# A gated DeltaNet scan whose small products go to all four quarters of TensorE's array, in two-bank PSUM tiles

## The chip, the cores and the metric

The kernel runs on one core of one Trainium2 chip. The metric is the device time of one execution in microseconds (us), as the median of the runs.

## What is computed

The reference is two layers of a mixer block with 1024 columns, over a context of 256 tokens and a latent stream of 1024. In each layer one normalised input goes through one input projection into four groups (a DeltaNet with short convolutions, a gated convolution, a Conformer convolution, a chunked spatial-gating MLP); their gated outputs are joined and go through one output projection with a gated residual. The change touches the DeltaNet: four heads of 64 columns, run forward and backward over chunks of 64 tokens (16 for the latent stream, 4 for the context). With the state S of a head and direction, a chunk does

```
x  = sg0 * (K S) + nk
v  = T x
o  = sg1 * (Q S) - A v
S  = sg2 * S + K' (sg3 * v)
```

K, Q and K' are the chunk's keys and queries, T the inverse of a triangular 64x64 matrix, A the causal weights of the chunk, sg0 to sg3 gates, nk the negated values. The context's last state starts the latent scan of its layer.

## The kernel before

The program is not written in the order in which it runs. Class `Program` records every operation, `estimate` (line 140) gives each a cost, and `schedule` (line 255) puts the operations of each engine into one fixed order: of those that are ready it takes the one with the smallest number of recording, less a boost (800 for the scan, `AHEAD_SCAN`; 600 for convolutions, 300 for the rest of the DeltaNet, 0 for the inversion). Since all operations are issued by one helper, every row of the profile shows line 214, and an operation is known by its tiles.

Most of TensorE's time goes to the dense projections (`mm3`, tiles `mm`): each is three products of 128x128 by 512 columns in a reduced fp32 format, on high and low parts (`hh`, `hl`). What the scan leaves of TensorE is filled with them.

The DeltaNet of a stream runs in stages, `gdn` (line 1310) first:

- `norms` (1417): sums of squares per token and head, by 64x1 products.
- `pair_matrices` (1444): for two chunks a call the products K K and Q K of both directions, masked. A call stores its `zd` (three matrices, one DMA each) and its `at` (two DMAs) to DRAM on SP's queue. There are 8 calls for a latent stream and 2 for a context, 20 in all.
- `invert` (1488): loads 32x32 blocks of `zd` (tile `u`), inverts them by a row loop on VectorE, and stores `zb`. It runs in two groups of chunks for the latent stream.
- `prep` in `scan` (1540): for four chunks, loads `zb`, `zd` and `at`, and makes the full 64x64 inverses T with 32x32 products (tile `ax<-b,b`).
- `scan` (1520): the loop over the chunks. The four scans of the program (context, latent; layer 0, layer 1) have 4, 16, 4 and 16 steps.
- `gdn_out` (1677), then the output projection (`out_item`), with weights from `load_w_out` (1717).

In the scan, the 128 partitions hold two heads' halves p, and an index hh picks the pair of heads; d is the direction. So each product of the formula is a group of eight 64x64 by 64 products, over d, hh and p. Half p of the rows writes half p of the PSUM partitions:

```
for d, hh, p in each:
    self.mm(A[half[p], 0, d, hh, :], st.qk[hh][half[p], 1, tok(d)], S[half[p], d, hh, :])
```

That is the two quarters on the diagonal of the array, in turn. A group in fp32 stands in the trace as 16 instructions, for each product is two passes. A step runs K S (`sc<-s,u`) into bank A; two VectorE operations make x; T x (`sc<-x,u`) goes into A too; a copy on ScalarE makes v1, VectorE makes v2; K' v2 (`sc<-v,u`) goes into its own bank, and VectorE adds it to gs into S. Beside that chain stand Q S and A v1 (into a bank Bk), VectorE's `at`, `ot` and `gs`, and the addition to the output. `psx` (517) hands out single PSUM banks to everything else: four banks of the scan and the bank `ax` in turn, or `ax` alone while a scan runs.

Of the kernel before, what the change touches and what calls it, by code (L numbers as in the profile page):

```python
# [16 lines left out]
P = 128  # L17
# [62 lines left out]
class Program:  # L80
# [13 lines left out]
    def __init__(self, nc):  # L94
        self.nc = nc
        self.ops, self.slots, self.hist, self.tileops, self.bufs = [], {}, {}, {}, {}
        self.masks, self.boost, self.joined = {}, 0, None
        self.tensor, self.vector = Engine(self, "PE", nc.tensor), Engine(self, "DVE", nc.vector)
        self.scalar, self.gpsimd = Engine(self, "ACT", nc.scalar), Engine(self, "POOL", nc.gpsimd)
        self.sync = Engine(self, "SP", nc.sync)  # L100
# [39 lines left out]
    def estimate(self, eng, method, out, ins, args, kw):  # L140
# [45 lines left out]
    def add(self, calls):  # L186
# [29 lines left out]
        for w, aps in ((False, ins), (True, outs)):  # L216
            for a in aps:
                name = a.name
                if "PSUM" in str(a.space):
                    reg, bank = (0, 128, 1), True  # L220
                elif name in self.slots or "DRAM" in str(a.space):
                    if name not in self.slots and not name.startswith(self.DRAM_OWN):
                        continue
                    reg, bank = self.region(a), False
                else:
                    continue
# [237 lines left out]
class Block:  # L464
    def __init__(self, es, tc, ins, out, dbg=None):
        self.tc, self.nc, self.i, self.out = tc, Program(tc.nc), ins, out
        pool = lambda name, bufs, **kw: es.enter_context(tc.tile_pool(name=name, bufs=bufs, **kw))
        self.cp = pool("cp", 1)
        self.sp = pool("sp", 2)
        self.hp = pool("hp", 1)  # L470
        self.pools = {k: pool(k + "p", n) for k, n in CAPS.items()}
        self.cnt = {k: 0 for k in CAPS}
        self.dp = pool("dp", 1, space=DRAM)
        self.mmp = pool("mm", 3, space=PSUM)
        self.ax = pool("ax", 1, space=PSUM)
        self.sc = pool("sc", 1, space=PSUM)
        self.n = self.xi = self.scanning = 0
        self.W = Weave()

# [44 lines left out]
    def scan_bank(self, k, shape):  # L524
        return self.nc.own(self.sc.tile(shape, F32, tag=f"sc{k}", name=self.nm("sc")), f"sc{k}", 1)

# [723 lines left out]
    def group_a_gates(self, st):  # L1250
# [3 lines left out]
        def ev(j):  # L1254
            def go(ps, b0, n):
# [4 lines left out]
                def put():  # L1260
                    for q in range(2):
                        r = q * P + j * HD
                        nc.sync.dma_start(st.gd[r:r + HD, b0:b0 + n], g[q * HD:(q + 1) * HD])
# [44 lines left out]


    def gdn(self, st, need_q, states):  # L1310
        nc, l, n = self.nc, st.l, st.n
# [30 lines left out]

        pe = self.psx([P, 6, m])
        for d in range(2):
            self.mm(pe[:, d], self.Rm[d], g[:, d])
            self.mm(pe[:, 2 + d], self.Lm[d], g[:, d])
# [19 lines left out]
        st.nk = V("nk", 1)[:, 0]  # L1366
        nc.vector.tensor_tensor(st.nk, nq[:, 1], rn[:, 1], ALU.mult)
        wd = S("wd", [P, 2, 32])[:, :, :m]
# [21 lines left out]
        for hh in range(2):  # L1390
            self.shuffle(st.nkv, st.pad, hh, n)
        if not st.ctx:
# [24 lines left out]
    def norms(self, st, kind, nq):  # L1417

        nc, n = self.nc, st.n
        pq = self.psx([P, 2 * n])  # L1420
        for b0, nb in st.blocks:
            for hh in range(2):
                yield self.room("b")
# [3 lines left out]
                for c in range(nb // TC):  # L1427
                    e = (b0 // TC + c) * 2 + hh
                    for p in range(2):
                        s = slice(p * TC, (p + 1) * TC)  # L1430
                        self.mm(pq[s, e:e + 1], sq[s, c * TC:(c + 1) * TC], self.ones[s])
                self.free("b")
        nc.vector.tensor_scalar(nq[:, kind], pq, EPS, None, ALU.add)

    def shuffle(self, dst, src, hh, n):

        for q in range(4):
            p, a = q // 2, q % 2
            v = src[q * CH:(q + 1) * CH, hh, 1:n * TC + 1].rearrange("p (c u j) -> p u c j", u=2, j=CH)
            for u in range(2):  # L1440
                r = p * TC + u * CH
# [78 lines left out]
    def scan(self, st, S, need_o):  # L1520
# [62 lines left out]

        pend = None

        def out(s, i, bank, v1, at):
            AT = ATs[s // G % 2]
            for d in range(2):
                for hh in range(2):
                    e = 2 * (G - 1 - i if d else i) + hh  # L1590
                    for p in range(2):
                        self.mm(bank[half[p], 1, d, hh, :], AT[half[p], d, e], v1[half[p], d, hh, :])

        def out_add(s, i, bank, v1, at):
            oc = st.o[:, two_of(s, n - 1 - s)].rearrange("p d (h e) -> p d h e", h=2)
# [6 lines left out]
            if not fresh:  # L1602
                self.two(oc, oc, ot, ALU.add)

        yield from prep(0)
        side = None
        for s in range(n):
# [4 lines left out]
            first, last = st.ctx and s == 0, s == n - 1 and not st.ctx  # L1612
            each = [(d, hh, p) for d in range(2) for hh in range(2) for p in range(2)]
            sg = lambda k: st.sg[:, s, k].unsqueeze(3).to_broadcast(sh)
            tok = lambda d: slice(cc[d] * TC, (cc[d] + 1) * TC)
            A = self.scan_bank(0, [P, 2, 2, 2, HD])
            nk = st.nkv[:, two_of(*cc)].rearrange("p d (h e) -> p d h e", h=2)
            if first:
                x = nk
            else:  # L1620
                for d, hh, p in each:
                    self.mm(A[half[p], 0, d, hh, :], st.qk[hh][half[p], 1, tok(d)], S[half[p], d, hh, :])
# [12 lines left out]
            nc.joined = None if first else ready  # L1635
            for d, hh, p in each:
                self.mm(A[half[p], 1, d, hh, :], Ts[j % 2][half[p], d, 2 * (G - 1 - i if d else i) + hh, :], x[half[p], d, hh, :])
            at = None
            if need_o:
                Bk = self.scan_bank(2, [P, 2, 2, 2, HD])  # L1640
                if not first:
                    for d, hh, p in each:
                        self.mm(Bk[half[p], 0, d, hh, :], st.qk[hh][half[p], 0, tok(d)], S[half[p], d, hh, :])
            if not last:
# [3 lines left out]
            if need_o:  # L1648
                v1 = self.small("v1", sh)
                nc.scalar.copy(v1, A[:, 1])  # L1650
                if not first:
                    at = self.small("at", sh)
                    nc.vector.tensor_tensor(at, Bk[:, 0], sg(1), ALU.mult)
                pend = (s, i, Bk, v1, at)
            yield STEP[1]
            if not last:
                nc.joined = ready
                Sp = self.scan_bank(1, sh)
                for d, hh, p in each:
                    self.mm(Sp[half[p], d, hh, :], st.kst[half[p], cc[d], hh * HD:(hh + 1) * HD], v2[half[p], d, hh, :])  # L1660
                if first:
                    nc.vector.tensor_copy(S, Sp)
                else:
                    nc.vector.tensor_tensor(S, gs, Sp, ALU.add)
            if side:
# [6 lines left out]
        if need_o:  # L1672
            out(*pend)
            out_add(*pend)
        self.scanning -= 1
# [41 lines left out]
    def load_w_out(self, l, after, keep):  # L1717
# [5 lines left out]
        for i, k in enumerate((4, 5, 6, 7, 2, 3, 0, 1)):  # L1723
            yield lambda: self.cnt["u"] + 1 + keep() <= CAPS["u"]
            r = raw[:, i % 2]
            if k < 2:
                for h in range(2):
                    r0 = (2 * h + k) * HD
                    nc.sync.dma_start(r[h * HD:(h + 1) * HD], self.i["w_out"][l, r0:r0 + HD, :])
# [403 lines left out]
```

## Time and profile before

| | |
|---|---|
| median of 3 runs | 1384.72 us (1384.66 to 1385.25) |
| the profiled execution | 1382.8 us, of which its span 1381.1 us |
| TensorE, weight loads, VectorE, ScalarE busy | 94%, 76%, 71%, 39% of the span |
| mean granted TensorE clock | 0.969 |

The profile is of one execution. Its span goes from the first instruction to the last. Matmuls overlap, and the busy time of one is its whole length, so that a TensorE shown busy can still have room. A latent scan of layer 0 stands at about 456 to 570 us and that of layer 1 at 1109 to 1206 us.

### The profile page before, as it was taken

The page shows a single profiled execution, that of the slowest core. Times are in us where ns is not written, and L with a number is a line of the kernel's source. Part 1 is how long each engine was busy: PE and PEld are TensorE (multiplying, and loading weights), DVE is VectorE, ACT ScalarE, POOL GpSimd, SP SyncE. Part 2 cuts the span into 40 slices and gives each one's busy share as a digit, 9 for nine tenths or more (in the row PEclk, how much of TensorE's full clock was granted, in tenths as well). Part 3 has the DMA queues.
Part 4 walks back from the last instruction along what each step waited for, and adds up shares of the span by engine and source line. Part 5 has one row for each costly group of instructions (what it writes and reads, how often), then busy time and mean ns, then how long its engine had stood idle before and what let it go on. Part 6 is the DMA issues. An engine that isn't in the chain of part 4 may idle for free.

```text
span 1381.1 us, 27009 instructions
## 1 busy us (share of the span) xinstructions
PE 1299.9 (94%) x10992; PEld 1047.1 (76%) x10992; DVE 986.2 (71%) x2102; ACT 539.9 (39%) x903; POOL 11.9 (1%) x76
## 2 busy tenths in 40 slices
PE   6887899999999999999999999998999888999997
PEld 4886778987778666678887788987777776788886
DVE  3888959999869755753466659899788866753554
ACT  4877433254644221321244355343475121231221
POOL 1000000000000000000000000000000000000000
PEclk9988899999999999999999999999899989999999
DMA  9748232322485566561333341523237533122831
GB/s 306 213 109 242 58 74 70 86 47 61 111 203 145 151 198 190 185 184 54 109 115 111 100 113 51 128 54 88 66 99 178 121 80 100 49 76 96 269 82 56
DMA packets 308465, 166.74 MB, mean 121 GB/s; under 512 B 148254, under 2 KB 292982, under 8 KB 308342
## 3 DMA queue, kind: packets, MB, share of 16 engines
q1 hardware_dynamic: 308342, 165.03, 43.3%
q8 instruction: 86, 1.41, 0.4%
q14 instruction: 37, 0.30, 0.1%
HBM read 124.32 MB, written 35.42 MB: 116 GB/s over the span
## 4 chain that ended last, share of the span: by engine, by line
PE 60%; DVE 15%; DMA 14%; ACT 3%; issue 3%; SPq 3%; ACTq 0%; DVEq 0%
PE mm L214 45%; PE sc L214 11%; DVE u L214 8%; DMA x<-u 6%; PE ax L214 5%; DVE b L214 3%; SPq L214 3%; DMA r<-in_w_in 3%; DVE w L214 2%; DMA u<-in_w_out 2%; ACT u L214 1%; DMA whh<-in_w_ada 1%; DMA whl<-in_w_ada 1%; DMA u<-in_x 1%; DMA b<-zb 1%
## 5 line engine op out<-in xcount | busy, mean ns | idle before, releaser
L214 PE MATMUL mm<-hh,w 128*128 128x512 f32 x1664 | 541.4, 401 | 1.7 <-ACT w L214 1.2
L214 PEld LDWEIGHTS mm<-hh,w 128*128 128x128 f32 x1664 | 311.8, 190 | 82.0 <-issue 16.5
L214 PE MATMUL mm<-hl,w 128*128 128x512 f32 x832 | 334.3, 402 | 0.0
L214 PE MATMUL mm<-u,w 128*128 128x512 f32 (+1 forms) x1320 | 261.5, 356 | 1.6 <-ACT g L214 1.1
L214 PEld LDWEIGHTS mm<-u,w 128*128 128x128 f32 x1320 | 220.0, 193 | 35.3 <-ACT g L214 1.7
L214 DVE SCALAR_TENSOR_TENSOR u<-u,pv,u 128x1024 f32<-128x1024 f32 (+1 forms) x172 | 201.9, 1182 | 1.0
L214 PEld LDWEIGHTS mm<-hl,w 128*128 128x128 f32 x832 | 157.9, 190 | 40.7 <-issue 9.3
L214 ACT CAST w<-r 128x1024 fp32r<-128x1024 f32 x88 | 92.5, 1051 | 214.4 <-PE mm L214 159.2
L214 ACT ACT_TABLE_LOAD x94 | 120.6, 1283 | 17.7 <-DMA zd<-b 5.9
L214 DVE TENSOR_TENSOR w<-r,w 128x1024 fp32r<-128x1024 f32 x88 | 107.2, 1218 | 27.3 <-ACT w L214 26.8
L214 DVE TENSOR_TENSOR u<-u,b 128x256 f32<-128x256 f32 (+25 forms) x246 | 89.3, 378 | 26.5 <-DMA u<-in_x 16.3
L214 PE MATMUL mm<-u,u 128*128 128x256 f32 (+1 forms) x384 | 56.5, 299 | 9.8 <-ACT u L214 4.2
L214 DVE TENSOR_TENSOR b<-u 128x108 f32<-128x108 f32 (+21 forms) x180 | 56.5, 323 | 7.0 <-DMA u<-zd 3.8
L214 PEld LDWEIGHTS mm<-u,u 128*128 128x128 f32 x384 | 51.2, 200 | 12.8 <-DVE u L214 5.0
L214 ACT ACTIVATE b<-u 128x512 f32<-128x512 f32 (+1 forms) x71 | 42.5, 609 | 40.4 <-DVE u L214 29.4
L214 PEld LDWEIGHTS sc<-v,u 64*64 64x64 f32 x1184 | 40.3, 138 | 16.0 <-DVE v L214 9.9
L214 PEld LDWEIGHTS sc<-s,u 64*64 64x64 f32 x1168 | 40.6, 141 | 15.1 <-DVE s L214 4.5
L214 PE MATMUL sc<-s,u 64*64 64x64 f32 x1168 | 47.3, 230 | 2.3 <-DVE u L214 1.7
L214 PE MATMUL sc<-v,u 64*64 64x64 f32 x1184 | 46.6, 226 | 2.5 <-DVE v L214 1.3
L214 PE MATMUL mm<-u,hh 128*128 128x272 f32 x256 | 48.5, 289 | 0.0
L214 ACT ACTIVATE b<-sc,mod,modG 128x128 f32<-128x128 f32 x76 | 30.9, 459 | 44.5 <-PE sc L214 26.9
L214 PE MATMUL sc<-dg,u 128*128 128x128 f32 x248 | 38.2, 311 | 8.7 <-issue 4.7
(271 smaller groups left out, 1451.8 us busy)
## 6 DMA issues: line engine op xcount, KB each, us to landing
r<-in_w_in SPq DMA_DIRECT2D x90, 512.0 KB
u<-in_w_ada SPq DMA_DIRECT2D x16, 1024.0 KB
u<-in_x SPq DMA_DIRECT2D x16, 512.0 KB
r<-ylat SPq DMA_DIRECT2D x16, 512.0 KB
zd<-b SPq DMA_DIRECT2D x60, 128.0 KB
ylat<-g SPq DMA_DIRECT2D x24, 256.0 KB
u<-in_w_out SPq DMA_DIRECT2D x12, 512.0 KB
at<-b SPq DMA_DIRECT2D x36, 128.0 KB
```

Of the source, the lines that this page charges most:

```text
L214: op.alts[e] = ((lambda fn=fn, ar=ar, k=k: fn(*ar, **k)), cost, table)
```

## The change

It does six things, all in the DeltaNet and the recording layer.

1. In the scan the heads with hh = 1 change sides: half p of the rows writes half 1 - p of the partitions for K S, Q S, T x and A v1. Over p and hh, four products in a row then go to four different quarters of the array. K' v2 stays on the diagonal.
2. Each PSUM tile of the scan is a pair of two banks, one bank for each hh. A holds two groups, Bk three (Q S, the output of the step before, K' v2). The pair A and the pair Bk are four banks, as before. Dependencies are tracked by bank.
3. Q S and the output of the step before are recorded ahead of T x.
4. What feeds the scan changes sides with it for hh = 1: norms get a tile and a VectorE operation for each hh, the gates' sums are split (four small products for two), the queries' scaling gets one more product and copy, and shuffles, gates and the rows of the output weights are permuted with as many DMAs as before.
5. The store of a `zd` matrix becomes three DMAs (one of 128 partitions, two of 64): 9 for a call where there were 3.
6. The scheduler's cost of an fp32 product of up to 64 rows or columns goes from max(0.15, 0.05 + n/600) to max(0.116, 0.01 + n/600) us, and is divided by four for the groups of item 1, by two for others on the diagonal.

```diff
@@ estimate
-                return max(0.15, 0.05 + n * 4 / 2400.0) / self.side_by_side(k, m)
+                return max(0.116, 0.01 + n * 4 / 2400.0) / (4 if self.quads else self.side_by_side(k, m))
@@ psx
-        self.xi = (self.xi + 1) % 5
-        if self.scanning or self.xi == 4:
-            return self.nc.own(self.ax.tile(shape, F32, tag="ax", name=self.nm("ax")), "ax", 1)
-        return self.scan_bank(self.xi, shape)
+        if self.scanning:
+            self.other = None
+        t, self.other = self.other, None
+        if t is None:
+            self.xi = (self.xi + 1) % 3
+            if self.scanning or self.xi == 2:
+                return self.nc.own(self.ax.tile(shape, F32, tag="ax", name=self.nm("ax")), "ax", 1)
+            pair = self.scan_pair(self.xi)
+            t, self.other = pair[:, 0], pair[:, 1]
...
+    def scan_pair(self, k):
+
+        return self.nc.own(self.sc.tile([P, 2, 512], F32, tag=f"sc{k}", name=self.nm("sc")), f"sc{k}", 1)
@@ norms
-        nc.vector.tensor_scalar(nq[:, kind], pq, EPS, None, ALU.add)
...
+            nc.vector.tensor_scalar(nq.rearrange("p k (c h) -> p k c h", h=2)[:, kind, :, hh], pq, EPS, None, ALU.add)
@@ pair_matrices
         for d, t in ((0, gx[:, 0]), (1, gx[:, 1]), (2, z)):
-            nc.sync.dma_start(zd[d, 2 * s0:2 * s0 + 4].rearrange("c p i -> p c i"), t)
+            to = zd[d, 2 * s0:2 * s0 + 4].rearrange("(c h) p i -> h p c i", h=2)
+            t = t.rearrange("p (c h) i -> p h c i", h=2)
+            nc.sync.dma_start(to[0], t[:, 0])
+            for p in range(2):
+                nc.sync.dma_start(to[1, (1 - p) * TC:(2 - p) * TC], t[p * TC:(p + 1) * TC, 1])
@@ scan
+        pair = lambda k, r: self.scan_pair(k)[:, :, 0:r * P].rearrange("p h (r d e) -> p r d h e", r=r, d=2)
+
+        def quads(calls):
+            nc.quads = True
+            for c in calls:
+                self.mm(*c)
+            nc.quads = False
...
+            A = pair(0, 2)
+            Bk = pair(1, 3) if need_o or not last else None
...
+            into = lambda bank, r, kind: quads((bank[half[p ^ hh], r, d, hh, :], st.qk[hh][half[p], kind, tok(d)],
+                                                S[half[p], d, hh, :]) for d, hh, p in each)
...
+            if need_o and not first:
+                into(Bk, 0, 0)
             if pend:
-                out(*pend)
-                out_add(*pend)
+                out(Bk, *pend)
+                out_add(Bk, *pend)
+            at = None
+            if need_o and not first:
+                at = self.small("at", sh)
+                nc.vector.tensor_tensor(at, Bk[:, 0], sg(1), ALU.mult)
...
+            quads((A[half[p], 1, d, hh, :], Ts[j % 2][half[p ^ hh], d, 2 * (G - 1 - i if d else i) + hh, :],
+                   x[half[p ^ hh], d, hh, :]) for d, hh, p in each)
...
-                Sp = self.scan_bank(1, sh)
                 for d, hh, p in each:
-                    self.mm(Sp[half[p], d, hh, :], st.kst[half[p], cc[d], hh * HD:(hh + 1) * HD], v2[half[p], d, hh, :])
+                    self.mm(Bk[half[p], 2, d, hh, :], st.kst[half[p], cc[d], hh * HD:(hh + 1) * HD], v2[half[p], d, hh, :])
```

The order of the instructions changes with it. On TensorE, one step of layer 0's context scan stood like this (tiles: `s` the state, `x`, `v1` and `v2` as in the formula, `mm` a dense product; the first row is K S, the second Q S):

```order
L214 MATMUL sc_309_406<-s_1_94,u_123_220 64x64 x8
L214 MATMUL sc_312_409<-s_1_94,u_123_220 64x64 x8
L214 MATMUL mm_355_452<-hl0_188,w_321_418 128x512
L214 MATMUL mm_355_452<-hh0_187,w_321_418 128x512 x2
L214 MATMUL sc_309_406<-x_310_407,u_124_221 64x64 x8
L214 MATMUL mm_355_452<-hl0_188,w_321_418 128x512
L214 MATMUL mm_355_452<-hh0_187,w_321_418 128x512 x2
L214 MATMUL sc_317_414<-v2_313_410,u_123_220 64x64 x8
L214 MATMUL sc_312_409<-v1_314_411,u_124_221 64x64 x8
L214 MATMUL mm_355_452<-hl0_188,w_321_418 128x512
```

and now stands like this, up to the update of the state:

```order
L215 MATMUL sc_298_395<-s_1_94,u_114_211 64x64 x8
L215 MATMUL sc_299_396<-s_1_94,u_114_211 64x64 x8
L215 MATMUL sc_299_396<-v1_296_393,u_115_212 64x64 x8
L215 MATMUL mm_342_439<-hh0_178,w_335_432 128x512 x2
L215 MATMUL mm_342_439<-hl0_179,w_335_432 128x512
L215 MATMUL mm_342_439<-hh0_178,w_335_432 128x512 x2
L215 MATMUL mm_342_439<-hl0_179,w_335_432 128x512
L215 MATMUL sc_298_395<-x_300_397,u_115_212 64x64 x8
L215 MATMUL mm_342_439<-hh0_178,w_335_432 128x512 x2
L215 MATMUL mm_342_439<-hl0_179,w_335_432 128x512
L215 MATMUL mm_342_439<-hh0_178,w_335_432 128x512
```

The output of the step before has moved ahead of the dense products, and more of these stand in a step: 7 before, 14 to 18 now in this scan. Over the whole program, counted from the first K S of a scan to its last step, 29 more stand in the latent scan of layer 0 and 65 more in that of layer 1 (71 before, 136 now), and as many fewer behind that one (697 before, 632 now); ahead of it their number is as before.

A late step of layer 1's latent scan, from T x to the next K S, before:

```order
L214 MATMUL sc_1482_1581<-x_1483_1582,u_1315_1414 64x64 x8
L214 MATMUL mm_1410_1509<-hl1_978,w_1370_1469 128x512
L214 MATMUL mm_1410_1509<-hh1_977,w_1370_1469 128x512 x2
L214 MATMUL sc_1493_1592<-v2_1487_1586,u_1140_1239 64x64 x8
L214 MATMUL sc_1486_1585<-v1_1488_1587,u_1315_1414 64x64 x8
L214 MATMUL mm_1410_1509<-hl1_978,w_1370_1469 128x512
L214 MATMUL sc_1494_1593<-s_1_94,u_1137_1236 64x64 x2
```

and now:

```order
L215 MATMUL sc_1383_1482<-x_1385_1484,u_1250_1349 64x64 x8
L215 MATMUL mm_1351_1450<-hh1_930,w_1331_1430 128x512
L215 MATMUL mm_1351_1450<-hl1_931,w_1331_1430 128x512
L215 MATMUL mm_1351_1450<-hh1_930,w_1331_1430 128x512 x2
L215 MATMUL sc_1384_1483<-v2_1389_1488,u_1084_1183 64x64 x8
L215 MATMUL mm_1351_1450<-hl1_931,w_1331_1430 128x512
L215 MATMUL mm_1351_1450<-hh1_930,w_1331_1430 128x512 x2
L215 MATMUL sc_1396_1495<-s_1_94,u_1081_1180 64x64 x2
```

The output product has left the place behind K' v2, and a dense product more stands in each of the two gaps.

On SP's queue, the stretch in which layer 0's latent pair matrices are stored (`zd`, `at`) and the inversion's first blocks are loaded (`u<-zd`) stood like this:

```order
L214 DMA zd_593<-b_594 128x4x64 x2
L214 DMA at_561<-b_595 128x256 x2
L214 DMA zd_593<-b_600 128x4x64
L214 DMA u_632<-u_505 32x16x32 x5
L214 DMA u_562<-zd_563 32x32x32 x2
L214 DMA gd_130<-g_630 64x512 x2
```

and the same stretch now:

```order
L215 DMA zd_566<-b_567 128x2x64
L215 DMA at_538<-b_568 128x256 x2
L215 DMA zd_566<-b_567 64x2x64 x2
L215 DMA zd_566<-b_567 128x2x64
L215 DMA zd_566<-b_567 64x2x64 x2
L215 DMA zd_566<-b_573 128x2x64
L215 DMA zd_566<-b_573 64x2x64 x2
```

A call holds 11 DMAs where it held 5, and the loads `u<-zd` of the first inversion, which stood between the calls, now stand behind the last of them.

## Rows read from the trace of the kernel before

**Rows 1.** The page: busy time of the engines, and the chain's shares by engine.

```profile
PE 1299.9 (94%) x10992; PEld 1047.1 (76%) x10992; DVE 986.2 (71%) x2102; ACT 539.9 (39%) x903; POOL 11.9 (1%) x76
...
PE 60%; DVE 15%; DMA 14%; ACT 3%; issue 3%; SPq 3%; ACTq 0%; DVEq 0%
```

**Rows 2.** Windows over the two latent scans; columns: length, busy of PE, PEld, DVE, ACT, POOL (count), clock, DMA share, GB/s.

```profile
456.00:570.00 114.00, 111.94 (x2098) 74.44 (x2100) 68.76 (x172) 23.73 (x57) 0.20 (x4) 0.99 0.62 180
1109.00:1206.00 97.00, 88.15 (x1754) 68.97 (x1755) 64.27 (x150) 23.45 (x49) 0.00 (x0) 0.93 0.29 76
```

**Rows 3.** Timeline, one scan step of layer 1: start, length, engine, operation.

```profile
1178.44 0.42 DVE L214 TENSOR_TENSOR s<-gs,sc 128x256 f32<-128x256 f32 x1 [0.78 <-PE sc L214]
1179.22 1.17 PE L214 MATMUL sc<-s,u 64*64 64x64 f32 x32
1180.04 0.41 DVE L214 TENSOR_TENSOR x<-sc,sg 128x256 f32<-128x256 f32 x1
1181.22 0.68 PE L214 MATMUL sc<-x,u 64*64 64x64 f32 x16
1181.99 0.37 ACT L214 COPY v<-sc 128x256 f32<-128x256 f32 x1 [4.79 <-PE sc L214]
1182.40 0.42 DVE L214 TENSOR_TENSOR v<-sc,sg 128x256 f32<-128x256 f32 x1 [1.16 <-ACT v L214]
1182.88 1.15 PE L214 MATMUL sc<-v,u 64*64 64x64 f32 x32
1183.60 0.42 DVE L214 TENSOR_TENSOR s<-gs,sc 128x256 f32<-128x256 f32 x1 [0.78 <-PE sc L214]
```

**Rows 4.** TensorE's groups by shape: count, busy us, mean ns of one, idle before.

```profile
L214 PE MATMUL sc<-s,u 64*64 64x64 f32 x1168 | 47.3, 230 | 2.3 <-DVE u L214 1.7 <-DVE s L214 0.5
L214 PE MATMUL sc<-v,u 64*64 64x64 f32 x1184 | 46.6, 226 | 2.5 <-DVE v L214 1.3
L214 PE MATMUL sc<-x,u 64*64 64x64 f32 x608 | 30.0, 230 | 3.1 <-ACT u L214 2.1 <-issue 0.6
L214 PE MATMUL ax<-u,cs 128*32 128x256 f32 x256 | 25.7, 388 | 0.0
L214 PE MATMUL ax<-b,b 32*32 32x32 f32 x1280 | 19.7, 204 | 13.0 <-issue 9.5 <-ACT u L214 2.4 <-DVE b L214 0.5
L214 PE MATMUL sc<-u,u 64*64 64x64 f32 x32 | 1.8, 271 | 0.0
```

**Rows 5.** Timeline of PE: 16 and 64 products in four tiles, 16 in two.

```profile
531.42 1.07 PE L214 MATMUL ax<-u,cs 128*32 128x256 f32 x16
...
974.51 0.68 PE L214 MATMUL sc<-x,u 64*64 64x64 f32 x16
...
1106.49 1.08 PE L214 MATMUL ax<-b,b 32*32 32x32 f32 x64 [0.52 <-ACT b L214]
```

**Rows 6.** Chain: the longest stretch of dense products (us, engine, tile, count).

```profile
604.21 80.70 PE mm L214 x355
```

**Rows 7.** The zd stores on SP's queue: ns min/median/max, first and last start.

```profile
L214 SPq DMA_DIRECT2D zd<-b x60: 360/470/1896, 92.5 to 1069.6; - x60
```

**Rows 8.** Chain ahead of the two latent scans.

```profile
425.37 1.60 SPq L214
444.61 5.33 DMA zb<-u
452.47 2.57 DMA b<-zb
...
1051.15 0.64 SPq L214
1051.89 2.23 DMA zd<-b
```

**Rows 9.** Timelines: SP in layer 0's pair matrices, PE ahead of layer 1's scan.

```profile
402.68 1.33 SPq L214 DMA_DIRECT2D zd<-b  x2
...
1104.79 1.19 PE L214 MATMUL ax<-b,b 32*32 32x32 f32 x64 [3.79 <-issue]
```

More of the change, by code (lines that the diff above doesn't have):

```diff
@@ L517, in psx @@
     def psx(self, shape):
[L519 to L525 removed]
+        if self.scanning:
+            self.other = None
+        t, self.other = self.other, None
[5 more added lines that the diff above has]
+            t, self.other = pair[:, 0], pair[:, 1]
+        n = 1
+        for x in shape[1:]:
+            n *= x
+        t = t[0:shape[0], 0:n]
+        if len(shape) == 3:
+            t = t.rearrange("p (a b) -> p a b", b=shape[2])
+        elif len(shape) == 4:
+            t = t.rearrange("p (a b c) -> p a b c", b=shape[2], c=shape[3])
+        return t
+    def scan_pair(self, k):
+        return self.nc.own(self.sc.tile([P, 2, 512], F32, tag=f"sc{k}", name=self.nm("sc")), f"sc{k}", 1)
     def mm(self, out, lhsT, rhs, start=True, stop=True):
@@ L1343, in gdn @@
         pe = self.psx([P, 6, m])
+        half = [slice(p * TC, (p + 1) * TC) for p in range(2)]
         for d in range(2):
-            self.mm(pe[:, d], self.Rm[d], g[:, d])
+            self.mm(pairs(pe)[:, d, :, 0], self.Rm[d], pairs(g)[:, d, :, 0])
+            for p in range(2):
+                self.mm(pairs(pe)[half[p], d, :, 1], self.Rm[d][:, half[1 - p]], pairs(g)[:, d, :, 1])
             self.mm(pe[:, 2 + d], self.Lm[d], g[:, d])
@@ L1366, in gdn @@
         st.nk = V("nk", 1)[:, 0]
-        nc.vector.tensor_tensor(st.nk, nq[:, 1], rn[:, 1], ALU.mult)
+        nc.vector.tensor_tensor(t[:, 1], nq[:, 1], rn[:, 1], ALU.mult)
+        pf = self.psx([P, 1, m])
+        self.mm(pairs(pf)[:, 0, :, 0], self.ident, pairs(t)[:, 1, :, 0])
+        for p in range(2):
+            self.mm(pairs(pf)[half[p], 0, :, 1], self.ident[:, half[1 - p]], pairs(t)[:, 1, :, 1])
+        nc.vector.tensor_copy(st.nk, pf[:, 0])
         wd = S("wd", [P, 2, 32])[:, :, :m]
@@ L1419, in norms @@
         nc, n = self.nc, st.n
-        pq = self.psx([P, 2 * n])
-        for b0, nb in st.blocks:
-            for hh in range(2):
+        for hh in range(2):
+            pq = self.psx([P, n])
+            for b0, nb in st.blocks:
                 yield self.room("b")
@@ L1584, in scan, with out, out_add @@
         pend = None
-        def out(s, i, bank, v1, at):
-            AT = ATs[s // G % 2]
[L1588 to L1594, printed above, removed]
+        pair = lambda k, r: self.scan_pair(k)[:, :, 0:r * P].rearrange("p h (r d e) -> p r d h e", r=r, d=2)
[4 more added lines that the diff above has]
+            nc.quads = False
+        def out(bank, s, i, v1, at):
+            AT = ATs[s // G % 2]
+            quads((bank[half[p ^ hh], 1, d, hh, :], AT[half[p], d, 2 * (G - 1 - i if d else i) + hh], v1[half[p], d, hh, :])
+                  for d, hh, p in each)
+        def out_add(bank, s, i, v1, at):
             oc = st.o[:, two_of(s, n - 1 - s)].rearrange("p d (h e) -> p d h e", h=2)
@@ L1603, in out_add @@
                 self.two(oc, oc, ot, ALU.add)
+        each = [(d, hh, p) for d in range(2) for hh in range(2) for p in range(2)]
         yield from prep(0)
@@ L1620, in scan @@
             else:
-                for d, hh, p in each:
-                    self.mm(A[half[p], 0, d, hh, :], st.qk[hh][half[p], 1, tok(d)], S[half[p], d, hh, :])
+                into(A, 0, 1)
                 x = self.small("x", sh)
@@ L1650, in scan @@
                 nc.scalar.copy(v1, A[:, 1])
[L1651 to L1654, printed above, removed]
+                pend = (s, i, v1, at)
             yield STEP[1]
@@ L1672, in scan @@
         if need_o:
-            out(*pend)
-            out_add(*pend)
+            Bk = pair(1, 3)
+            out(Bk, *pend)
+            out_add(Bk, *pend)
         self.scanning -= 1
```

38 lines of the change are left out of this document (16 added, 22 removed).

## The prediction

> **What bounds the kernel now.** I read the page first: TensorE is busy for 94% of the span and holds 60% of the chain, VectorE and DMA some 15% each, SP's queue 3% [rows 1]. A reader should not stop there, for the busy time of a product is its whole length. The longest stretch of the chain shows the real pace of the dense products: 355 in 80.70 us, 0.227 us each [rows 6]. So in most of the kernel the end comes when these products are done, and a change gains if it takes other work off TensorE, or lets dense products into time in which TensorE waits.
>
> Such time lies in the scans. In the windows over the two latent scans TensorE is shown busy for 111.94 of 114 us and for 88.15 of 97 [rows 2], but the timeline of one step tells more. From one update of the state to the next it takes 1183.60 - 1178.44 = 5.16 us [rows 3]. Two groups that run together take 1.15 to 1.17 us for 32 instructions, one alone 0.68 for 16 [rows 3], so that a further group costs 1.16 - 0.68 = 0.48, by instructions 0.0294 us each and **0.47 us a group**; the rest of the 0.68 is the time that the last product takes to come out. Five groups (2.35 us) and the 7 dense products of this step (1.59) make 3.94 us: 1.2 us stay empty. The step is bound by its chain: state, K S, two operations for x, T x, ScalarE's copy, v2, K' v2, state [rows 3].
>
> Ahead of the scan lies another chain, through SP and VectorE: SP's queue at 425.37, the store of the inverse at 444.61 (5.33 us to land) and its load at 452.47 in layer 0, SP's queue and a `zd` store at 1051.15 and 1051.89 in layer 1 [rows 8]. There the scan's first `prep` on TensorE had to wait, 3.79 us of idle time ahead of 1104.79 [rows 9].
>
> **The four quarters.** Counts: 1168, 608 and 1184 instructions by 16 [rows 4] make 73 groups of K S and Q S, 38 of T x with 2 more in the two first steps (32 instructions that read `u` [rows 4]), and 74 with v, of which 38 are K' v2 and 36 the output. 73 + 40 + 36 = 149 groups go to four quarters, 38 stay. No row shows 64x64 products in four quarters, where two row halves write the same output half at once. Bounds: no gain at all (0.47 a group), and a time in proportion to the quarters (0.235). Near rows: 64 products in four 32x32 tiles took 1.08 us of which one lasts 0.204, so (1.08 - 0.20)/63 = 14.0 ns each [rows 4, 5]; 16 products of 128x32 by 256, four column tiles that share all rows, took 1.07 us with 0.388 for one, 45 ns each [rows 4, 5]. They show that four tiles do run together, the second though all share rows. I take 0.235, nearest to the first of these. On TensorE that is 149 x 0.235 = 35.0 us.
>
> On the chain, K S and T x are each 0.235 shorter, so 0.47 a step: 5.16 becomes 4.69. 15 steps in each latent scan give 2 x 7.05 us.
>
> A rule weighs against this. The two-tile and four-tile rows above show loads and products overlapping at 29 and 14 ns. The Trainium skill (TensorE: Matmul & The Clock Gate, "What overlaps and what doesn't") says that a weight load overlaps a product in flight only where its row group differs. The order hh, p alternates two row halves, as before, so by that rule a group would stay at 0.47 us and the 35 us would be 0. The column tiles at 45 ns, which share their rows, speak against the rule here.
>
> **The dense products in the scans.** The order shows 29 more in layer 0's latent scan and 65 more in layer 1's, with as many fewer behind the latter. At 0.227 us [rows 6] they are worth 6.6 and 14.8 us if they fit. Room in a new step: from the end of K S to T x 1181.22 - 1179.22 - 0.47 = 1.53, less Q S and the output 1.06; from T x to K' v2 1.66 - 0.47 = 1.19; from there to the next K S about 1.03; together 3.28 us or 14 products [rows 3, 6]. Late steps hold 10 to 16. Gaps filled beyond their room add some 2 us in each scan, and half as much again for those filled to the brim: I take 3 us off each. Latent scans: -(7.05 + 6.6 - 3) = -10.7 and -(7.05 + 14.8 - 3) = -18.9. Layer 0's context scan has 3 full steps with 10.5 more dense products (2.4 us), and its gaps are overfull by 0.8: 5.16 + 2.4 - (4.69 + 0.8) = 2.1, three times -6.2. Layer 1's context scan has its dense products as before; 7 groups shorter by 0.235 give -1.6. Together **-37.4 us**.
>
> **The reordered step.** K' v2 now writes a bank that VectorE reads for `at` and `ot`, and waits for both. They stand ahead of v2 on VectorE, so v2 is later anyway. But `ot`, `at` and the addition now stand between x and v2: 3 x 0.42 = 1.26 us. From x to v2 lie 0.32 (to T x), the copy's start 0.77 - 0.235 after it, and 0.41 of the copy [rows 3], 1.27 together. A tie, taken as nothing; up to 0.2 us a step in 35 steps (7 us) if it is later.
>
> **The stores.** 20 calls issue 6 more DMAs each, 120 in all. A `zd` store holds SP's queue for 0.470 us (median; 0.360 to 1.896) [rows 7]: 56.4 us of queue. For a latent stream it is 48 x 0.47 = 22.6, for a context 5.6. Behind them on SP wait the loads for the inversion, `at`, gates and weights. Bounds of the delay: nothing, where the queue was idle between the calls, and all 56.4. For nothing speaks that a call's matrices come from VectorE, whose pace may leave SP room; against it that in this stretch the queue is full of other DMAs (two stores took 1.33 us at 402.68 [rows 9]), that it lies on the chain in both layers [rows 8], and that the first inversion's loads now stand behind the last call. At the least the last call is 6 x 0.47 = 2.8 us later. I take a third of the 22.6 for each latent stream, 7.6, and 1 for each context, nearer to the lower end: **+17.2**. An inversion that is later moves `prep` and the scan with it; TensorE already ran out of dense work there [rows 9].
>
> **The rest.** Norms, split gate sums and the extra product and copy add some 11 VectorE operations at 0.1 to 0.4 us and a few products for the four scans; +1.3 on the chain ahead of the scans. PSUM outside the scan: five single banks as before, but handed out in pairs; nothing, with a copy's 0.4 us now and then as its upper end. The scheduler's cheaper cost has no price of its own: it is in the counts.
>
> Sum: -37.4 + 17.2 + 1.3 = -18.9. The profiled execution took 1382.8, 1.9 less than the median. 1382.8 - 18.9 = 1363.9; with the 1.9, **1365.8, so 1366 us**.
>
> **Rivals.**
>
> *Quarters that share rows or columns don't run at once*, so the change doesn't do what it says. A group stays at 0.47, a step at 5.16, and dense products put into it make it as much longer as they shorten the end: gain 0, cost 17.2 + 1.3, so 1403 us. The rule of the Trainium skill above is this case. For: no row shows this use of the array. Against: both four-tile rows [rows 5]. Chance 0.10.
>
> *SP's queue takes it all back* (the other side). The mechanism: SP issues in order, the loads `u<-zd` and `b<-zb` wait behind stores, VectorE's inversion starts late, the scan with it. It decides from a delay of 37.4 - 1.3 = 36.1 us on, that is 0.64 of the 56.4; with all of it 1366 + 39 = 1405. For: the queue is on both chains [rows 8]. Against: SP's queue holds only 3% of the chain [rows 1], some 41 us in all, and a call's stores come only when VectorE has made its matrices. Chance 0.10.
>
> *SP hides the stores.* The inversion's row loop on VectorE and not SP's queue is what ends last; 1366 - 17 = 1349. For: the inversion's loads are few and the two inversions run beside each other anyway. Chance 0.17.
>
> *Overfull steps.* The order is fixed by a cost model; where it lays more products into a gap than fit, K S, T x and K' v2 are late, and VectorE's tie adds 7 us. Half the dense gain goes (10.7): 1366 + 18 = 1384. Chance 0.10.
>
> **How the numbers follow.** Forecast 0.53 (1366, own range 1354 to 1378), SP hidden 0.17, quarters 0.10, SP in full 0.10, overfull 0.10. Some 0.2% of the time, 2.8 us, is what a measurement can tell from no change. Faster: 0.53 + 0.17 + 0.06 of the overfull case = 0.76. Within 0.2%: 0.03 of that case and 0.03 of part of SP's = 0.06. Slower: the rest, 0.18. The range leaves out the upper parts of the two slow cases (0.14) and a tail below: 1340 to 1396.
>
> **What would show it.** Four quarters: 16 instructions of `sc<-x` in about 0.45 us instead of 0.68, and K S to x shorter by 0.235. Steps: 4.7 us late in layer 1's latent scan, 9 to 13 dense products in each. SP: the first load `u<-zd` of a latent inversion against its last `pair_matrices` call, and the idle time of TensorE ahead of the scan's first `prep`; some 8 us more in each layer. The prediction is wrong if a group stays near 0.47, if steps don't get shorter though groups do (then a wait of VectorE or a gap holds them), or if the scans start as early as before, or more than 15 us later.

## The result, and the profile after

The changed kernel takes 1407.41 us (median of 4 runs, 1400.71 to 1408.71), the kernel before beside it 1384.69. The ratio is 1.0148, with a 95% interval of 1.0117 to 1.0178: it is slower by 1.5%, where the forecast was 1366 us and its range 1340 to 1396. The profiled execution took 1408.71 us, its span 1407.0, 25.9 more than the span before.

The page first, its busy times and the chain by engine [rows 1]:

```profile
PE 1286.8 (91%) x11048; PEld 1020.7 (73%) x11048; DVE 985.0 (70%) x2105; ACT 541.2 (38%) x908; POOL 11.9 (1%) x76
...
PE 67%; DMA 9%; DVE 9%; SPq 6%; ACT 5%; issue 3%; DVEq 0%; ACTq 0%
```

TensorE is busy for 13 us less, and SP's queue has gone from 3% to 6% of the chain. TensorE's groups by shape and the `zd` stores on SP's queue say both in figures [rows 4, 7]:

```profile
L215 PE MATMUL sc<-v,u 64*64 64x64 f32 x1184 | 42.2, 225 | 2.7 <-DVE v L215 1.9 <-issue 0.4
L215 PE MATMUL sc<-s,u 64*64 64x64 f32 x1168 | 27.3, 231 | 0.2 <-DVE s L215 0.2
L215 PE MATMUL sc<-x,u 64*64 64x64 f32 x608 | 20.6, 234 | 3.3 <-issue 3.0
```

```profile
L215 SPq DMA_DIRECT2D zd<-b x180: 366/588/2072, 94.2 to 1116.6; - x180
```

The groups of K S and Q S fell from 47.3 to 27.3 us at the same count. There are three times as many stores, and in the median one holds the queue for 0.588 us against 0.470: 0.541 for those of 128x2x64 and 0.601 for those of 64x2x64. Added up, the `zd` stores hold SP's queue for 110.2 us where they held it for 33.7, and the 120 of 64x2x64 alone for 75.8.

One late step of layer 1's latent scan, from the timeline [rows 3]:

```profile
1208.47 0.42 DVE L215 TENSOR_TENSOR s<-gs,sc 128x256 f32<-128x256 f32 x1 [0.78 <-PE sc L215]
...
1209.25 0.69 PE L215 MATMUL sc<-s,u 64*64 64x64 f32 x32
...
1209.78 0.42 DVE L215 TENSOR_TENSOR x<-sc,sg 128x256 f32<-128x256 f32 x1 [0.42 <-PE sc L215]
...
1211.01 0.46 PE L215 MATMUL sc<-x,u 64*64 64x64 f32 x16
...
1211.58 0.37 ACT L215 COPY v<-sc 128x256 f32<-128x256 f32 x1 [3.79 <-PE sc L215]
...
1211.99 0.43 DVE L215 TENSOR_TENSOR v<-sc,sg 128x256 f32<-128x256 f32 x1 [0.21 <-ACT v L215]
...
1212.75 0.68 PE L215 MATMUL sc<-v,u 64*64 64x64 f32 x16
...
1213.48 0.42 DVE L215 TENSOR_TENSOR s<-gs,sc 128x256 f32<-128x256 f32 x1 [1.07 <-PE sc L215]
```

Two groups take 0.69 us where they took 1.17, one takes 0.46 where it took 0.68. From K S to x it is 0.53 (0.82 before), from T x to the copy 0.57 (0.77): the chain of this step is 0.49 us shorter, where 0.47 was forecast. K' v2, still on the diagonal (0.68), starts 0.33 after v2 has ended (0.06 before), because five dense products fill the gap. So this step takes 5.01 us with 11 products instead of 5.16 with 7. It is one of the shortest: the 14 steps between the updates of this scan take 5.42 us each in the mean, where they took 5.88.

The kernel as a whole is settled elsewhere. The table is made from the starts of VectorE's rows that update S, 38 in each trace, and from the counts of dense products between them in the order (in units of 512 columns). "Left over" is the change in length, less 0.227 us [rows 6] for each product that moved in or out.

| stretch | before | after | products | left over |
|---|---|---|---|---|
| to the first update, layer 0's context | 194.4 | 208.4 | +38 | +5.4 |
| that scan | 15.5 | 18.8 | +28 | -3.1 |
| to layer 0's latent scan | 253.5 | 262.4 | -52 | +20.7 |
| that scan | 102.8 | 101.8 | +30 | -7.8 |
| to layer 1's context scan | 405.1 | 408.9 | -20 | +8.3 |
| that scan | 18.4 | 18.2 | -12 | +2.5 |
| to layer 1's latent scan | 128.3 | 147.0 | -13 | +21.7 |
| that scan | 82.3 | 75.8 | +60 | -20.1 |
| to the end | 180.8 | 165.7 | -58 | -1.9 |

The four scans gained 28.5 us and the end 1.9; the four stretches ahead of the scans lost 56.1. The windows over 380 to 440 us, where layer 0's latent pair matrices are made, show it on every engine. The columns are those of [rows 2]; the first row is of the kernel before, the second of the changed one:

```profile
380.00:440.00 60.00, 57.64 (x395) 46.22 (x394) 46.00 (x118) 29.74 (x35) 0.31 (x2) 0.94 0.73 179
```

```profile
380.00:440.00 60.00, 46.47 (x361) 34.80 (x360) 29.88 (x52) 21.77 (x25) 0.00 (x0) 0.88 0.54 116
```

VectorE, which makes the matrices, falls from 46 to 30 us of the 60. It does less because it waits, so it is not what bounds this stretch. The chain of the same 60 us, by line, before and after:

```profile
by line: SPq L214 25.2%; PE mm L214 18.1%; DVE u L214 11.3%; DVE b L214 9.2%; PE sc L214 9.2%; DMA at<-b 8.6%; issue 5.7%; DMA gd<-g 4.4%; ACT L214 2.1%; DMA b<-in_b_ada 1.9%; DVE g L214 1.2%; ACT u L214 1.0%; ACT b L214 1.0%; ACT g L214 1.
```

```profile
by line: SPq L215 55.6%; issue 12.3%; DMA zd<-b 9.9%; DVE b L215 8.7%; DMA gd<-g 5.0%; ACT L215 4.3%; DMA at<-b 4.0%; ACT b L215 2.0%; ACT g L215 1.0%; ACTq L215 0.3%; DVEq L215 0.2%
```

And SP's queue there, from its timeline, hardly ever idle (in the 60 us its rows fill 54.8, before 45.8):

```profile
413.23 1.02 SPq L215 DMA_DIRECT2D at<-b  x2
414.30 5.91 SPq L215 DMA_DIRECT2D zd<-b  x8
420.25 0.63 SPq L215 DMA_DIRECT2D u<-u  x1
420.98 0.57 SPq L215 DMA_DIRECT2D zd<-b  x1
421.64 0.91 SPq L215 DMA_DIRECT2D at<-b  x2
422.60 3.16 SPq L215 DMA_DIRECT2D zd<-b  x5
...
429.76 2.02 SPq L215 DMA_DIRECT2D u<-zd  x3
```

A call's buffers are free for the next only when its stores have landed (in these 60 us VectorE waits 4.0 us for `zd<-b` to land and ScalarE 5.8), so a full queue sets the pace of the calls, and the inversion's loads `u<-zd` come when the last is through. The first update of layer 0's latent scan comes at 489.6 us instead of 463.4, that of layer 1's at 1165.5 instead of 1117.9.

### The profile page after: what moved, and what is told of

Same layout as the page of the kernel before. It is cut to its first block, busy times and chain, and to the rows that moved or that the text cites. A ratio compares the mean times of both kernels' runs of the same rounds, so it can differ in the third digit from the quotient of the medians.

```text
span 1407.0 us, 27315 instructions
## 1 busy us (share of the span) xinstructions
PE 1286.8 (91%) x11048; PEld 1020.7 (73%) x11048; DVE 985.0 (70%) x2105; ACT 541.2 (38%) x908; POOL 11.9 (1%) x76
## 4 chain that ended last, share of the span: by engine, by line
PE 67%; DMA 9%; DVE 9%; SPq 6%; ACT 5%; issue 3%; DVEq 0%; ACTq 0%
PE mm L215 51%; PE sc L215 10%; SPq L215 6%; PE ax L215 6%; DVE u L215 4%; DVE b L215 4%; DMA r<-in_w_in 3%; ACT u L215 2%; ACT L215 1%; DMA zd<-b 1%; DMA x<-u 1%; ACT b L215 1%; DVE w L215 1%; ACT w L215 1%; DMA zb<-u 1%
## 5 line engine op out<-in xcount | busy, mean ns | idle before, releaser
L215 PE MATMUL mm<-hh,w 128*128 128x512 f32 x1664 | 549.2, 406 | 12.0 <-ACT g L215 10.7
L215 PEld LDWEIGHTS mm<-hh,w 128*128 128x128 f32 x1664 | 314.6, 192 | 94.1 <-issue 17.2
L215 PE MATMUL mm<-hl,w 128*128 128x512 f32 x832 | 338.1, 406 | 0.0
L215 DVE TENSOR_TENSOR u<-u,b 128x256 f32<-128x256 f32 (+26 forms) x246 | 90.0, 386 | 11.8 <-DMA u<-in_x 5.3
L215 PE MATMUL mm<-u,u 128*128 128x256 f32 (+1 forms) x384 | 62.6, 318 | 7.9 <-ACT g L215 5.6
L215 DVE TENSOR_TENSOR b<-u 128x220 f32<-128x220 f32 (+24 forms) x180 | 56.6, 330 | 11.6 <-DMA u<-zd 8.2
L215 PEld LDWEIGHTS mm<-u,u 128*128 128x128 f32 x384 | 55.9, 217 | 11.8 <-ACT g L215 6.0
L215 PE MATMUL sc<-dg,u 128*128 128x128 f32 x264 | 41.0, 306 | 18.9 <-ACT b L215 11.1
L215 PEld LDWEIGHTS sc<-dg,u 128*128 128x128 f32 x264 | 37.5, 215 | 22.9 <-ACT b L215 12.8
L215 PEld LDWEIGHTS sc<-v,u 64*64 64x64 f32 x1184 | 33.6, 137 | 16.4 <-DVE v L215 10.8
L215 PE MATMUL sc<-v,u 64*64 64x64 f32 x1184 | 42.2, 225 | 2.7 <-DVE v L215 1.9
L215 ACT COPY v<-sc 128x256 f32<-128x256 f32 x36 | 13.4, 372 | 80.1 <-PE sc L215 66.1
```

What stands on the lines that cost most here:

```text
L215: op.alts[e] = ((lambda fn=fn, ar=ar, k=k: fn(*ar, **k)), cost, table)
```

## The experiments

The theory after this reading: SP's stores took back the gain (S). Its rivals: the paired banks, the layout work or the planned order (Q). Each run was compared with the kernel before on the same chip, whose median was between 1384.8 and 1386.7.

**Three stores in the changed kernel, and nine in the kernel before.** The first, three_zd, leaves out the exchange of halves in `zd`, and so do three_diag, three_diag_cost2, three_old_cost and three_plain below: their times serve to compare, and are not times of the whole computation.

```diff
-            nc.sync.dma_start(to[0], t[:, 0])
-            for p in range(2):
-                nc.sync.dma_start(to[1, (1 - p) * TC:(2 - p) * TC], t[p * TC:(p + 1) * TC, 1])
+            nc.sync.dma_start(zd[d, 2 * s0:2 * s0 + 4].rearrange("c p i -> p c i"), t)
```

> The changed kernel with the zd stores of before: three DMAs a call instead of nine. The two halves of heads 2 and 3 are then not exchanged in zd, so this part of the layout, and with it these heads' T, is left as before. Theory S (SP's queue): in the changed kernel the stretches ahead of the four scans are 56 us longer than their dense work explains, and 120 stores at 0.47 us are 56 us; without them these stretches go back and the time is 1408 - 56 = 1352 us, within 8. Rival Q (the stall has another cause: the paired PSUM banks outside the scan, the norms' extra steps, the order): the time stays over 1390 us.

> The kernel before with nine zd stores a call, split as in the change (without the exchange of halves). Theory S: 120 more DMAs on SP's queue ahead of the scans and nothing else; 1385 + 56 = 1441 us, and by the 0.6 us that such a store holds the queue up to 1457. Rival Q: the queue has room for them, below 1395 us.

Measured: 1368.68 us (ratio 0.9876, 0.985 to 0.9903) and 1433.66 (1.0347, 1.0321 to 1.0372). Taking 120 stores away gives back 38.7 us, adding them costs 49. S holds in both directions, but at less than its 56, and both times lie outside what it gave (1344 to 1360, and 1441 to 1457): the rest of the 56.1 is not the stores'. Divided as in the table above, three_zd's trace still loses 14.8 us ahead of the scans: 6.1 to the first update, 4.4 and 4.5 in layer 1, and nothing (-0.2) ahead of layer 0's latent scan. The windows of three_zd and of before_nine_zd over the same 60 us fall on either side:

```profile
380.00:440.00 60.00, 56.47 (x401) 44.58 (x400) 49.10 (x126) 30.19 (x36) 0.32 (x2) 0.94 0.74 180
```

```profile
380.00:440.00 60.00, 47.76 (x338) 37.81 (x337) 35.97 (x76) 20.98 (x25) 0.16 (x1) 0.88 0.59 137
```

VectorE has 46 to 49 us of work with three stores and 30 to 36 with nine, in either kernel.

**Two quarters instead of four**, in three_zd: `bank[half[p ^ hh], ...]` becomes `bank[half[p], ...]` in K S, Q S and the output, and T and x are read from `half[p]`.

> The kernel three_zd with the outputs of all heads in the scan written to their own half again, so that the products go to two quarters in turn; banks, order of recording and the scheduler's cost stay those of the change. The heads 2 and 3 are then not computed rightly. If the four quarters are worth what the groups show (0.27 us less for each of 149 groups, two of them on the chain of each step), it is 20 to 40 us slower than three_zd. If the shorter groups are swallowed by other waits of the step, the two are within 8 us.

Measured: 1395.74 us (1.0066, 1.0042 to 1.0091), 27.1 slower than three_zd. The groups by shape, of three_diag and then of three_zd:

```profile
L215 PE MATMUL sc<-s,u 64*64 64x64 f32 x1168 | 43.5, 224 | 0.2 <-DVE b L215 0.2
L215 PE MATMUL sc<-x,u 64*64 64x64 f32 x608 | 29.5, 227 | 1.9 <-ACT u L215 1.1 <-issue 0.8
```

```profile
L215 PE MATMUL sc<-s,u 64*64 64x64 f32 x1168 | 27.6, 233 | 1.5 <-DVE b L215 1.5
L215 PE MATMUL sc<-x,u 64*64 64x64 f32 x608 | 20.8, 234 | 1.6 <-issue 1.2 <-ACT u L215 0.3
```

(43.5 - 27.6)/73 = 0.22 us a group and (29.5 - 20.8)/38 = 0.23, with nearly the same order on TensorE in the scans: products in four quarters overlap as those in two don't. Of the 33.4 us between the two profiles (three_diag's is the slowest of its ten) 20.2 lie in the scans and 11.6 ahead of them. The run also shows that all the rest of the change, with three stores and in an order planned for four quarters, costs 11 us against the kernel before.

**The exchange of halves put elsewhere.** flip_in_prep keeps three stores and writes T's blocks to the other half for hh = 1:

```diff
-                            nc.sync.dma_start(T[blk(p, b), 0, :, b * CH:(b + 1) * CH], zv[blk(p, b), ss])
+                            for h in range(2):
+                                nc.sync.dma_start(T[blk(p ^ h, b), 0, h::2, b * CH:(b + 1) * CH],
+                                                  zv[blk(p, b), ss.start + h:ss.stop:2])
...
-                    self.copy(T[blk(p, b), 1, :, b * CH:(b + 1) * CH], CT[blk(p, b), 1])
+                    for h in range(2):
+                        self.copy(T[blk(p ^ h, b), 1, h::2, b * CH:(b + 1) * CH], CT[blk(p, b), 1, h::2])
```

and likewise for the copies from `pt`.

> The change with three zd stores a call, the halves of heads 2 and 3 being exchanged where T is put together in prep: four more loads a prep (40 in all) and eight more copies. Theory S: most of what three_zd gains stays, since in most preps this lies beside the scan; a first prep of a scan is 2 us (4 x 0.47) to 4 us later, four times: 1352 + 12 = 1364 us, 1355 to 1375. Rival Q: over 1390 us.

> flip_in_prep with the diagonal blocks of the forward direction copied on chip instead of loaded: 80 DMAs fewer than there (8 a prep), 40 fewer than in the kernel before, and 8 copies more a prep. Theory S: SP's loads stood on the chain ahead of each scan's first prep, 8 at 0.47 = 3.8 us of queue, and copies of about 0.3 us on two engines take 1 to 2 us of it back; 1375 - 4 x 2 = 1367 us, 1362 to 1375. Rival: the copies, which wait for one another on ScalarE and VectorE, make it slower than flip_in_prep, over 1378.

> flip_in_prep with the two at stores of a call as one DMA, by another order of at in DRAM: 18 DMAs fewer on SP. Theory S: 0.3 us to 0.4 us a store on the path, as 39 us for 120 and 49 us for 120 have shown, so 5 to 7 us: 1366 to 1371 us. Rival: three stores and two of at already leave SP room between calls, 1373 to 1378.

Measured: flip_in_prep 1375.45 us (0.9919, 0.9889 to 0.995), half a microsecond above what was expected and faster than both kernels. flip_copies took 1381.31 (0.9951, 0.9925 to 0.9978) and flip_at 1388.51 (1.0019, 1.0002 to 1.0036). Both took DMAs off SP and both became slower, so S fell here. flip_copies ended where its rival, the waiting copies, had put it, but its trace doesn't show that they are the cause: it differs from flip_in_prep's by 1.1 us ahead of the scans and 1.6 in them. flip_at fell on neither side. Its profile, the fastest of its twelve, loses 20.9 us ahead of the scans, 4.8 less than flip_in_prep, and gains only 21.0 in them instead of 29.7. So with three stores a call, what a DMA less on SP wins can be lost again in the scans. I take flip_at's 13 us as what another planned order can do by itself; no run shows that alone, and differences of that size are weak evidence.

**Another queue.** `nc.sync` becomes `nc.scalar` or `nc.gpsimd` for stores of `zd`, and the scheduler counts them as DMAs there.

> The change, with the 120 half stores of heads 2 and 3 issued by ScalarE on its own DMA queue instead of by SP; 60 stores stay on SP. Same bytes, same number, same pieces. Theory S (SP's serial issue): most of the 39 us that three_zd took off comes off again, less what ScalarE loses by issuing; 1370 to 1390 us. Rival L (small stores land late wherever they are issued, and the buffers of a call wait for that): 1400 us or more.

> As zd_act, but the 120 half stores are issued by GpSimd, which is busy for 1% of the span. Theory S: 1365 to 1385 us, if GpSimd issues a store in about the time between two of them (6 a call, a call some 6 us). Rival L: 1400 us or more.

> The change with all 180 zd stores issued by GpSimd, where zd_pool moved 120. GpSimd then holds 9 x 0.59 = 5.3 us of a call's time, about a call's pace. Theory S: no better than zd_pool's 1375, for one full queue has taken the place of another; 1370 to 1390. Rival: SP still bounds in zd_pool, 1360 to 1370.

> flip_in_prep with its 60 zd stores issued by GpSimd instead of SP. Theory S: SP's queue was full already in the kernel before, so that taking 60 more stores off it (28 us of queue) moves the scans further ahead; 1375 - 5 to 15 = 1360 to 1370 us. Rival: with three stores a call SP no longer ends last ahead of the scans, 1372 to 1378.

Measured: zd_act 1396.99 us (1.0066, 1.0042 to 1.009), zd_pool 1375.33 (0.9912, 0.9879 to 0.9944), zd_pool_all 1387.28 (1.0001, 0.998 to 1.0022), flip_pool 1430.41 (1.0306, 1.0271 to 1.0341). On an idle engine's queue the same 120 stores with the same bytes leave the kernel within 7 us of three_zd, so it is the issuing queue and not the landing of small stores (L falls). zd_act lies between S's 1390 and L's 1400. ScalarE's queue has its own work to hold up: the stores took 0.62 us each there in the median, 78.7 in all, and from 405.37 to 409.54 us, while six of them go out, no other instruction of ScalarE starts. How much of zd_act's time that makes was not tried. zd_pool_all came out as expected. flip_pool fell on neither side; GpSimd's timelines show why, zd_pool first, flip_pool second:

```profile
396.41 3.51 POOL L215 DMA_DIRECT2D zd<-b  x6 [0.51 <-DVE b L215]
406.16 3.51 POOL L215 DMA_DIRECT2D zd<-b  x6 [6.24 <-DVE b L215]
```

```profile
405.11 0.75 POOL L215 DMA_DIRECT2D zd<-b  x1 [1.97 <-DVE b L215]
408.47 0.76 POOL L215 DMA_DIRECT2D zd<-b  x1 [2.61 <-issue]
412.21 0.75 POOL L215 DMA_DIRECT2D zd<-b  x1 [2.98 <-issue]
415.68 0.76 POOL L215 DMA_DIRECT2D zd<-b  x1 [2.72 <-issue]
```

Six stores of 64x2x64 follow each other in 3.51 us, but a whole store of 128x4x64 is followed by the next only 3.4 to 3.7 us later, with no wait that the profile shows.

The division of the table above tells what sets these runs apart. In the changed kernel, in three_zd and in the seven runs that put the exchange or the stores elsewhere the scans gain 26 to 30 us (in flip_at 21.0). Ahead of them three_zd loses 14.8 us, flip_at 20.9, zd_pool 22.1, flip_in_prep 25.7, flip_copies 26.8, zd_pool_all 33.6, zd_act 43.7, the change 56.1 and flip_pool 80.0.

**What the order does by itself.** The scheduler's old cost in three_zd, its new cost in the kernel before, and the right cost (a half) in three_diag:

> three_zd (four quarters, three stores) with the scheduler's cost of before, 0.157 us and a half for each small product. It lays fewer dense products into the scans, 93 and 98 instead of 122 and 124 in the latent ones. The halves in zd are as in three_zd. If the packing is worth what the prediction gave it (0.227 us for each product moved into a step with room), it is some 55 x 0.227 = 12 us slower than three_zd, 1376 to 1384. If the steps of three_zd are overfull, so that products in them cost what they save, the two are within 4 us.

> The kernel before with the change's lower cost of a small fp32 product in the scheduler, and nothing else: two quarters, single banks. It tells what the order alone does. Theory P (the products in the scans follow from the shorter steps of the change): without shorter groups the order moves few products, and the time is 1380 to 1388 us. Rival (the cost table alone put more dense work into a step's 1.2 us of room): more than 20 products move into the two latent scans and the time is 1368 to 1380.

> three_diag (products in two quarters, three stores) with the order planned for two quarters: the scheduler counts a group's products at half cost each, not a quarter. Heads 2 and 3 are not computed rightly. three_diag was 11 us slower than the kernel before, though it has that kernel's products and stores. Theory O: these 11 us come from an order that lays more dense products into a step than fit beside two-quarter groups; with the right cost the time is 1380 to 1388 us. Rival: they come from the banks, the layout or the reordered step, and stay: 1392 us or more.

Measured: three_old_cost 1388.13 us (1.0012, 0.9993 to 1.0031), 19.5 slower than three_zd, more than either side expected. All four scans together hold 251 dense products between their updates there and 336 in three_zd, and last 219.3 and 223.4 us. So 85 products more make the scans 4.1 us longer and spare 85 x 0.227 = 19.3 elsewhere: 15.2 us gained, 0.18 for a product moved into a step. The other 4 of the 19.5 lie ahead of the scans (18.5 us lost there against 14.8). before_new_cost took 1388.9 (1.001, 0.9987 to 1.0032), the same as before: without shorter groups the cost table alone brings nothing. Yet its trace loses 10.2 us ahead of the scans, by its order alone. three_diag_cost2 took 1403.24 (1.0122, 1.0094 to 1.0149): an order planned for two quarters doesn't take the 11 us of three_diag away.

**The layout work, and the paired banks.** three_plain undoes the layout work ahead of the scan; before_pairs gives the kernel before the paired banks.

> three_zd without the work that carries the exchange of halves ahead of the scan: norms in one tile and one operation, the gates' sums in two products, no extra product and copy for the negated keys' scaling. The values of heads 2 and 3 are then wrong. Theory: these small operations cost some 1 to 2 us, as predicted; 1365 to 1370 us. Rival: they lie on the chain ahead of each scan and cost 3 us or more for each of four, under 1358.

> The kernel before with the PSUM banks of the scan handed out in pairs, outside the scan as in the change, and in the scan one half for A and the two halves of the other pair for the bank of Q S and the output and for the state's product. Order of recording, quarters, stores and costs stay. It tells what remains of three_zd's missing 17 us (1369 measured, 1352 expected). Theory N: handing out pairs costs nothing, 1380 to 1390 us. Rival P: a pair comes free only when both halves have been read, so that products outside the scan wait for copies; the first state update of the context scan, at 194 us in the kernel before and 208 in three_zd, comes 5 us or more later, and the time is over 1392.

Measured: three_plain 1370.21 us (0.9878, 0.9847 to 0.9908), the same as three_zd: the layout work costs nothing at the end. (Its first state update comes at 191.9 us, three_zd's at 207.9, but it loses 8.0 and 7.7 us ahead of layer 1's scans instead of 4.4 and 4.5.) before_pairs took 1413.14 (1.0189, 1.016 to 1.0218), over 1392 as rival P said, but not where P put it. Its first state update came at 197.2 us, and its longer time lies in the scans: layer 0's latent scan took 128.3 us instead of 102.8, layer 1's 93.5 instead of 82.3. There my edit ties the bank of Q S and the output to that of the state's product in one pair, which comes free a step later; the change doesn't do that. I read this cause from the edit; no run shows it. Ahead of the scans its trace loses nothing (-2.1 us in sum). So it shows no cost of pairs outside the scan, and doesn't settle what they cost in it.

## Why the prediction was wrong

- **The four quarters**: right. 0.235 us a group was forecast, 0.22 to 0.23 measured; on the chain 0.47 a step, measured 0.49 in the step shown. The rule of the Trainium skill (TensorE: Matmul & The Clock Gate, "What overlaps and what doesn't"), by which a group would have stayed at 0.47 us, does not hold for these quarters. For K S, Q S and the output the same two row halves alternate in three_diag and three_zd, and only the output half differs; T x now takes the row halves in the order 0, 1, 1, 0, and gains as much. That rival fell.
- **The dense products in the scans**: right in kind; three_old_cost shows a gain of 0.18 us each, not 0.227. The scans as a whole gained 28.5 us and not the 37.4 of the sum: the context scans gave -3.1 and +2.5 where -6.2 and -1.6 stood, the layer 0 latent scan -7.8 instead of -10.7; layer 1's was right (-20.1 against -18.9).
- **The reordered step**: VectorE's tie was one in the step shown, where v2 waited 0.21 us for the copy and not for VectorE. What came late there was K' v2, behind the dense products.
- **The stores**: this is the step that failed. "I take a third of the 22.6 for each latent stream, 7.6, and 1 for each context, nearer to the lower end: +17.2" was 38.7 in three_zd and 49 in before_nine_zd. Two things were wrong. A store was priced at the 0.470 us of a whole one, and a split one holds the queue for 0.588, so that SP's queue has 76.5 us more to issue and not 56.4. And the share of the delay was chosen from SP's 3% of the whole chain, an average over 1381 us, where the chain of 380 to 440 us would have shown SP's queue in first place with 25.2% already before. Added to a queue that comes first in its stretch, half to two thirds of that issue time came through (38.7 and 49 of 76.5), where the forecast had let 17.2 of 56.4 through. The prediction's own sign, scans that start more than 15 us later, is met: 26 us in layer 0 and 48 in layer 1.
- **The rival that came true** is SP's queue that takes it all back: it was to decide from a delay of 36.1 us and to end at 1405; measured 1407. It stood at a chance of 0.10, outweighed by the same reading of 3%. Its mechanism is shown; that its number is so near is luck, for it took a gain of 37.4 and a loss of 56.4, and the runs show 30.4 (scans and end), 38.7 for the stores, and 17 more lost ahead of the scans for another reason.
- **The rest**: +1.3 can't be told from nothing: three_plain, without that work, comes out like three_zd (ratios 0.9878 and 0.9876). But of the 56.1 us ahead of the scans 38.7 are the stores; the other 17, at nothing in the sum, stay open. Taking the layout work out doesn't win them back, and three_diag and three_diag_cost2 carry something of that size (11 and 18 us) with neither stores nor quarters. The planned order is the nearest candidate, since before_new_cost loses 10.2 us there by its order alone, but in the changed kernel it was not told apart from the paired banks in their own form.

## What to carry to other kernels

Before DMAs are added to a queue, take the chain of the stretch in which they are issued: where the queue was first there, each of them cost more than half of its issue time (here 0.32 to 0.41 us for each of 120, at some 0.6 us of queue), whatever the queue's share of the whole kernel. A layout that saves an engine work should be paid for where an idle engine or queue can carry it: the same four quarters gain 0.8% with the exchange made where T is put together (flip_in_prep; its variants 0.5% and nothing), and 0.9% with the half stores on GpSimd's queue. Read first how fast that queue takes stores of the shape: with whole stores on GpSimd's the kernel lost 3.1%.

## What was not expected

Stores over half of the partitions hold SP's queue longer than the whole ones (0.601 against 0.470 us in the median), and ScalarE's for 0.62. On GpSimd's queue, stores of 64x2x64 followed each other every 0.59 us and those of 128x4x64 only every 3.5 us, while in zd_pool_all the next store followed one of 128x2x64 after 0.73. And the clock fell where TensorE waited: in 380 to 440 us, with TensorE busy for 46.47 us instead of 57.64, the granted clock was at 1.2 GHz for 14 us instead of 7 and at 2.4 for the rest, 0.88 in the mean instead of 0.94; in the whole run 0.952 instead of 0.969. What this costs beside the waiting itself was not measured.
